# Batched attention-value product on one core: the loop of TensorE runs to the third unit from the end, and six of nine held stores go to the ring of SyncE

## The chip, the cores and the metric

One core of a Trainium2 chip. The metric is the device time of one execution in microseconds (us). A profiled execution has a span that is 1.8 us shorter than its time; moments below ("at 1046.2") count from the start of that span. "Landing" means a semaphore step that a DMA engine makes when its part of a transfer is done; a transfer over 16 engines makes 16, and the trace records each, without the engine's number.

In the views PE is TensorE, PEld its weight loads, DVE VectorE, ACT ScalarE, POOL GpSimd and SP SyncE (a q after the name: its queue of instructions), and L129 is line 129 of the kernel. The *ring* or *queue* of an engine holds the transfers that it has issued. GpSimd's *drain* (`pool.drain()`) is the last instruction of its program before the closing barrier.

## The reference

```python
batch, n_heads, seq, head_dim = 8, 12, 1024, 64      # float32
return np.einsum('bhqs,bhsd->bhqd', attn_weights, v)
```

The attention weights are 403 MB, v and the output 25 MB each.

## The kernel before

Two heads make a unit; there are NP = 48. GpSimd loads a unit with a cast to bf16 into one of two buffers. TensorE transposes it (64 matmuls of 128x128), VectorE and ScalarE copy the transposes out of PSUM, TensorE spreads v over the partitions by small matmuls and multiplies. A *plain* unit multiplies with v stationary, and its result is transposed back a unit later. A *direct* unit (the last three) multiplies group by group with the transposed weights stationary, so its result needs no transpose back and leaves in pieces.

```python
DIRECT = NP - 3          # units 45, 46, 47 are direct
LOOPED = DIRECT - 1      # units 2 to 43 in TensorE's loop, 0, 1 and 44 written out
HELD = 9                 # stores of units 38 to 46 wait behind the last loads
pieces_of = {NP - 4: [(0, GH), (GH, GH)], NP - 3: [(0, GH), (GH, GH)],
             NP - 2: [(0, 4), (4, 4), (8, 4), (12, 4)],
             NP - 1: [(0, 4), (4, 4), (8, 4), (12, 2), (14, 1), (15, 1)]}
last_stores = {4: (0, 8), 8: (8, 4), 12: (12, 2), 14: (14, 2)}
# ... (cut)
pe_pair(0, 1, 0, {0: (s_abf[0], 16)}, (s_vcast, 1), first=True)
pe_pair(1, 1, 1, {0: (s_abf[1], 16)}, None)
with nc.Fori(1, LOOPED // 2, 1, engines=(PE,)) as it:      # two units a turn
    # ...
for p in range(LOOPED, DIRECT): ...   pe_pair(...)         # unit 44
for p in range(DIRECT, NP):           pe_direct(p)         # units 45, 46, 47
# ... GpSimd:
for p in range(NP - 2):
    pool.wait_ge(s_t[True], (p + 1) * PER_DVE)   # unit p transposed: its buffer is free
    # ... v load after every odd unit
    load_attn(p + 2)
    if 0 < p <= HELD_FROM:
        store(p - 1)
for p in range(HELD_FROM, NP - 1):
    store(p)                                     # nine held stores, GpSimd's queue
pool.drain()
# ... SyncE: v's first load, four stores of unit 47, then waits for every store
```

Of the kernel before, what the change touches and what calls it, by code (L numbers as in the profile page):

```python
# [10 lines left out]
def kernel(  # L11
# [17 lines left out]
    nc = tc.nc  # L29
# [19 lines left out]

    DIRECT = NP - 3  # L50
    LOOPED = DIRECT - 1

    HELD = 9
    NO = HELD + 3
    pieces_of = {
        NP - 4: [(0, GH), (GH, GH)],
        NP - 3: [(0, GH), (GH, GH)],
        NP - 2: [(0, 4), (4, 4), (8, 4), (12, 4)],
        NP - 1: [(0, 4), (4, 4), (8, 4), (12, 2), (14, 1), (15, 1)],
    }  # L60

    groups_of = {p: [(0, 4), (4, 4), (8, 4), (12, 4)] for p in range(DIRECT, NP - 1)}
    groups_of[NP - 1] = [(0, 4), (4, 4), (8, 4), (12, 2), (14, 2)]
    last_stores = {4: (0, 8), 8: (8, 4), 12: (12, 2), 14: (14, 2)}
# [8 lines left out]
    def sem(name):  # L73
        return tc.alloc_semaphore(name)
# [8 lines left out]
    with tc.tile_critical(no_gpsimd_drain=True):  # L83
# [6 lines left out]
        vr = sb("vr", [P, VB, SB * D], bf16)  # L90
        vr_last = sb("vr_last", [P, VB, SB * D], bf16)
        vbf = [sb(f"vbf{i}", [P, SB, 2, D], bf16) for i in range(2)]
# [8 lines left out]
        s_abf = [sem(f"s_abf{i}") for i in range(2)]  # L101
        s_piece = {(p, n): sem(f"s_piece{p}_{n}") for p in pieces_of for n in range(len(pieces_of[p]))}
        s_v0, s_v, s_vlast = sem("s_v0"), sem("s_v"), sem("s_vlast")
        s_osb = [sem(f"s_osb{i}") for i in range(NO)]
# [6 lines left out]

        s_cp = [[sem(f"s_cp{i}_{g}") for g in range(G - 4)] for i in range(2)]
        s_vbf = [[sem(f"s_vbf{i}_{h}") for h in range(2)] for i in range(2)]
        s_ot = [[sem(f"s_ot{i}_{h}") for h in range(2)] for i in range(2)]

        s_c = {True: sem("s_c_dve"), False: sem("s_c_act")}
        s_out, s_od, s_oa = sem("s_out"), sem("s_od"), sem("s_oa")
        s_memset, s_const, s_vcast = sem("s_memset"), sem("s_const"), sem("s_vcast")

        def vr_of(p):  # L120
            return vr_last if p // 2 == NV - 1 else vr

# [15 lines left out]

        def spread_v(i, source):

            for h in range(2):
                rows = ds((2 * i + h) * VP, VP)
                for b in range(VB):
                    last = pe.matmul(  # L144
                        out=po[h],
                        lhsT=spread[rows, b],
                        rhs=source[rows, b],
                        start=(b == 0),
                        stop=(b == VB - 1),
                    )  # L150
                last.then_inc(s_sp[h])
# [29 lines left out]

        def pe_pair(i, n, before, waits, wait_v, first=False):

            for g in range(G):
                if g in waits:
                    pe.wait_ge(*waits[g])
                if g >= 4:
                    pe.wait_ge(s_cp[i][g - 4], n)
                transpose_g(abf[i], g)
            if not first:  # L190
                for h in range(2):
                    pe.wait_ge(s_ot[1 - i][h], before)
            if wait_v is not None:
                pe.wait_ge(*wait_v)
            spread_v(i, vr)
            if not first:
                transpose_back()
            for h in range(2):
                pe.wait_ge(s_vbf[i][h], n)
            multiply(i)  # L200

        def pe_direct(p):
# [5 lines left out]
            def mul(g):  # L208
# [8 lines left out]
                if g == 0:  # L217
                    for h in range(2):
                        pe.wait_ge(s_vbf[i][h], p // 2 + 1)
                copied = (p - DIRECT) * (PER_DVE if on_dve(g) else PER_ACT) + count_of(g)  # L220
# [16 lines left out]
            for g in range(G):  # L237
                if g in starts:

                    if g % 4 == 0:  # L240
                        while done < g:
                            mul(done)
                            done += 1
                    pe.wait_ge(s_piece[p, starts[g]], 16)
                if p > DIRECT or g >= 4:
# [4 lines left out]
                if g == 3:  # L250
                    if p == DIRECT:
                        for h in range(2):
                            pe.wait_ge(s_ot[1 - i][h], (p - 1) // 2 + 1)
                    elif p == NP - 2:
                        pe.wait_ge(s_vlast, 16)
                    spread_v(i, vr_of(p))
                    if p == DIRECT:
                        transpose_back()
# [6 lines left out]

        def piece_waits(p):
            return {g0: (s_piece[p, n], 16) for n, (g0, gn) in enumerate(pieces_of[p])}

        pe.wait_ge(s_const, 1 + VH)
        pe_pair(0, 1, 0, {0: (s_abf[0], 16)}, (s_vcast, 1), first=True)  # L270
        pe_pair(1, 1, 1, {0: (s_abf[1], 16)}, None)
        with nc.Fori(1, LOOPED // 2, 1, engines=(PE,)) as it:
            n = pe.snap(it + 1)
            loaded = pe.snap(it * 16)
            twice = pe.snap(loaded + 16)
            pe_pair(0, n, it, {0: (s_abf[0], twice)}, (s_v, loaded))
            pe_pair(1, n, n, {0: (s_abf[1], twice)}, None)
        for p in range(LOOPED, DIRECT):
            wait_v = (s_v, 16 * (p // 2)) if p % 2 == 0 else None
            pe_pair(p % 2, p // 2 + 1, (p - 1) // 2 + 1, piece_waits(p), wait_v)  # L280
        for p in range(DIRECT, NP):
# [3 lines left out]
        def copies_of_pair(p, dve):  # L285
# [7 lines left out]
            def spread_copy():  # L293
                eng.wait_ge(s_sp[h], p + 1)
                copy(  # L295
                    out=vbf[i][:, :, h], in_=po[h].rearrange("p (k d) -> p k d", k=SB)
                ).then_inc(s_vbf[i][h])

# [15 lines left out]
            for g in range(G):  # L314
# [3 lines left out]
                if on_dve(g) == dve:  # L318
# [5 lines left out]
                    if direct:  # L324
                        ins.then_inc(s_c[dve])
                    elif g < G - 4:
                        ins.then_inc(s_cp[i][g])
                if direct and g == 3:
# [13 lines left out]
        def back_copies(p):  # L342
            halves = osb[p % NO].rearrange("p (half j) d -> p half j d", half=2)
            free_osb(nc.scalar, p)
            for n in range(2):
                nc.scalar.wait_ge(s_back, 2 * p + n + 1)
                last = nc.scalar.copy(  # L347
# [5 lines left out]
        def ot_copy(p, h):  # L353
# [4 lines left out]
                out=ot[:, :, h], in_=po[h].rearrange("p (j q) -> p j q", j=GH)  # L358
            ).then_inc(s_ot[p % 2][h])

        nc.vector.memset(ident, 0.0).then_inc(s_memset)
        nc.vector.memset(spread, 0.0).then_inc(s_memset)
        nc.vector.wait_ge(s_v0, 16)
        nc.vector.tensor_copy(out=vr, in_=v32).then_inc(s_vcast)
        for p in range(NP):
# [13 lines left out]
        def load_attn(p):  # L379
            for n, (g0, gn) in enumerate(pieces_of.get(p, [(0, G)])):  # L380
                pool.dma_start(  # L381
                    out=abf[p % 2][:, ds(g0, gn)].rearrange("p g s -> p (g s)"),
                    in_=attn_p[p][:, ds(g0 * S, gn * S)],
                ).then_inc(s_piece[p, n] if p in pieces_of else s_abf[p % 2], 16)

        def load_v(iv):
            pool.dma_start(  # L387
                out=vr_of(2 * iv).rearrange("p b x -> p (b x)"), in_=v_g[iv]
            ).then_inc(s_v if iv < NV - 1 else s_vlast, 16)

        def store(p):
            if p < DIRECT:
                pool.wait_ge(s_out, p + 1)
            else:
                for s in (s_od, s_oa):
                    pool.wait_ge(s, (p - DIRECT + 1) * len(groups_of[DIRECT]))
            pool.dma_start(  # L397
                out=out_p[p].rearrange("p g d -> p (g d)"),
                in_=osb[p % NO].rearrange("p g d -> p (g d)"),
                single_packet=True,  # L400
            ).then_inc(s_osb[p % NO], 16)

# [25 lines left out]
        for p in range(NP - 2):  # L428
            pool.wait_ge(s_t[True], (p + 1) * PER_DVE)
            if p % 2 == 1 and (p + 1) // 2 < NV - 1:  # L430
                pool.wait_ge(s_sp[1], p + 1)  # L431
                load_v((p + 1) // 2)
            load_attn(p + 2)
            if p == LOOPED - 1:
                load_v(NV - 1)
            if 0 < p <= HELD_FROM:
                store(p - 1)
        for p in range(HELD_FROM, NP - 1):
            store(p)
# [3 lines left out]
        nc.sync.dma_start(out=v32.rearrange("p b x -> p (b x)"), in_=v_g[0]).then_inc(s_v0, 16)  # L443
        base = (NP - 1 - DIRECT) * len(groups_of[DIRECT])
        for k, (g0, gn) in enumerate(groups_of[NP - 1]):
            if g0 in last_stores:
                for s in (s_od, s_oa):
                    nc.sync.wait_ge(s, base + k + 1)
                gs = ds(*last_stores[g0])
                nc.sync.dma_start(  # L450
                    out=out_p[NP - 1][:, gs], in_=osb[(NP - 1) % NO][:, gs]
                ).then_inc(s_end, 16)
        for p in range(NP - 1 - NO, NP - 1):
            nc.sync.wait_ge(s_osb[p % NO], 16 * (p // NO + 1))
        nc.sync.wait_ge(s_end, 16 * len(last_stores))

# [29 lines left out]
```

## Time and profile before

| | before |
|---|---|
| time, median of the first three runs | 1059.7 us (1059.06 to 1059.75) |
| span of the profiled run | 1057.9 us |
| HBM read and written | 427.82 + 25.17 MB |
| TensorE busy | 75% |

The prediction below shows the lines that carry the reading. In the queue table a row is "queue kind: packets, MB, share of 16 engines". q0 is GpSimd's queue and q1 SyncE's. In the same table of the page of before:

```profile
q8 instruction: 9, 0.15, 0.1%
```

Those are nine packets of 16 KB. That they are TensorE's code is an inference: they come and go with the length of TensorE's program, as the experiments show.

### The profile page before, as it was taken

The page shows a single profiled execution, that of the slowest core. Times are in us where ns is not written, and L with a number is a line of the kernel's source. Part 1 is how long each engine was busy: PE and PEld are TensorE (multiplying, and loading weights), DVE is VectorE, ACT ScalarE, POOL GpSimd, SP SyncE. Part 2 cuts the span into 40 slices and gives each one's busy share as a digit, 9 for nine tenths or more (in the row PEclk, how much of TensorE's full clock was granted, in tenths as well). Part 3 has the DMA queues.
Part 4 walks back from the last instruction along what each step waited for, and adds up shares of the span by engine and source line. Part 5 has one row for each costly group of instructions (what it writes and reads, how often), then busy time and mean ns, then how long its engine had stood idle before and what let it go on. Part 6 is the DMA issues. An engine that isn't in the chain of part 4 may idle for free.

```text
span 1057.9 us, 12833 instructions
## 1 busy us (share of the span) xinstructions
PE 791.0 (75%) x5640; PEld 634.7 (60%) x5640; DVE 391.8 (37%) x589; ACT 397.3 (38%) x485; POOL 71.0 (7%) x137
## 2 busy tenths in 40 slices
PE   0896687866878678776787777876878768787995
PEld 0775476645755567555675556655666547656785
DVE  0443343333433334433353333433344334344452
ACT  0343343433433334433343333433344334344542
POOL 1010000100001000000000000000001000000020
PEclk9898888888889888898898888988789888898998
DMA  9999999999999999999999999999999999999997
GB/s 218 219 219 217 237 232 223 223 228 243 219 233 222 228 231 234 221 234 228 231 221 234 221 236 232 223 223 227 242 222 231 223 235 224 217 218 216 212 217 255
DMA packets 19171, 239.84 MB, mean 227 GB/s; under 512 B 2128, under 2 KB 2512, under 8 KB 11984
## 3 DMA queue, kind: packets, MB, share of 16 engines
q0 software_dynamic: 18432, 238.03, 100.1%
q1 hardware_dynamic: 720, 1.57, 0.4%
q8 instruction: 9, 0.15, 0.1%
q14 instruction: 10, 0.08, 0.0%
HBM read 427.82 MB, written 25.17 MB: 428 GB/s over the span
## 4 chain that ended last, share of the span: by engine, by line
DMA 66%; PE 29%; issue 1%; POOL 1%; ACT 1%; DVE 0%; POOLq 0%; SPq 0%
DMA abf<-in_attn_weights_dram 66%; PE bank L129 23%; PE bank L144 2%; PE bank L225 2%; POOL vr L387 1%; PE bank L172 1%; ACT at L320 0%; PE bank L156 0%; DVE vbf L295 0%; DVE at L320 0%; DVE osb L307 0%; ACT osb L347 0%; ACT vbf L295 0%; POOL abf L381 0%; POOLq L431 0%
## 5 line engine op out<-in xcount | busy, mean ns | idle before, releaser
L129 PE MATMUL bank<-ident,abf 128*128 128x128 f32 x3072 | 465.0, 322 | 249.7 <-DMA abf<-in_attn_weights_dram 249.7
L129 PEld LDWEIGHTS bank<-ident,abf 128*128 128x128 f32 x3072 | 453.0, 215 | 272.0 <-DMA abf<-in_attn_weights_dram 246.5
L320 DVE COPY at<-bank 128x1024 bf16<-128x1024 bf16 x480 | 320.5, 689 | 469.6 <-PE bank L129 466.1
L320 ACT COPY at<-bank 128x1024 bf16<-128x1024 bf16 x288 | 289.2, 1012 | 421.0 <-PE bank L129 421.0
L172 PE MATMUL bank<-at,vbf 128*64 128x512 bf16 x1440 | 216.5, 391 | 0.8 <-DVE vbf L295 0.8
L172 PEld LDWEIGHTS bank<-at,vbf 128*64 128x64 bf16 x1440 | 106.5, 108 | 96.2 <-DVE vbf L295 7.7
L357 ACT COPY ot<-bank 128x512 f32<-128x512 f32 x45 | 26.4, 587 | 183.7 <-PE bank L172 183.7
L357 DVE COPY ot<-bank 128x512 f32<-128x512 f32 x45 | 31.1, 692 | 144.5 <-PE bank L172 144.5
L381 POOL DMA_DIRECT2D abf<-in_attn_weights_dram x58 | 31.0, 539 | 423.8 <-PE bank L129 422.5
L156 PEld LDWEIGHTS bank<-ident,ot 128*128 128x128 f32 x360 | 38.5, 140 | 19.1 <-issue 19.1
L156 PE MATMUL bank<-ident,ot 128*128 128x128 f32 x360 | 49.2, 280 | 0.0
L347 ACT COPY osb<-bank 128x512 f32<-128x512 f32 x90 | 48.3, 589 | 0.3
L144 PE MATMUL bank<-vr,spread 32*128 32x512 bf16 x368 | 48.1, 377 | 0.0
L387 POOL DMA_DIRECT2D vr<-in_v_dram x22 | 11.6, 527 | 474.0 <-PE bank L144 474.0
L295 DVE CAST vbf<-bank 128x512 bf16<-128x512 f32 x48 | 33.2, 692 | 14.6 <-PE bank L144 14.6
L295 ACT CAST vbf<-bank 128x512 bf16<-128x512 f32 x48 | 28.1, 586 | 22.3 <-PE bank L144 22.2
L225 PE MATMUL bank<-vbf,at 128*128 128x128 bf16 x384 | 26.4, 219 | 4.4 <-DVE vbf L295 1.9
L397 POOL DMA_DIRECT2D out_dram<-osb x47 | 25.1, 543 | 59.5 <-ACT osb L347 48.3
L225 PEld LDWEIGHTS bank<-vbf,at 128*128 128x128 bf16 x384 | 22.9, 98 | 7.3 <-issue 2.9
L144 PEld LDWEIGHTS bank<-vr,spread 32*128 32x128 bf16 x368 | 15.4, 92 | 15.7
L307 DVE COPY osb<-bank 64x256 f32<-64x256 f32 (+1 forms) x13 | 5.1, 395 | 20.5 <-PE bank L225 20.5
L307 ACT COPY osb<-bank 64x256 f32<-64x256 f32 (+1 forms) x13 | 4.6, 351 | 20.6 <-PE bank L225 20.6
(13 smaller groups left out, 9.8 us busy)
## 6 DMA issues: line engine op xcount, KB each, us to landing
abf<-in_attn_weights_dram POOLq DMA_DIRECT2D x44, 4096.0 KB, 32.3
out_dram<-osb POOLq DMA_DIRECT2D x47, 512.0 KB, 32.3
vr<-in_v_dram POOLq DMA_DIRECT2D x22, 512.0 KB, 12.7
abf<-in_attn_weights_dram POOLq DMA_DIRECT2D x4, 2048.0 KB, 25.8
abf<-in_attn_weights_dram POOLq DMA_DIRECT2D x7, 1024.0 KB, 24.4
v<-in_v_dram SPq DMA_DIRECT2D x1, 1024.0 KB, 4.7
vr_last<-in_v_dram POOLq DMA_DIRECT2D x1, 512.0 KB, 30.3
abf<-in_attn_weights_dram POOLq DMA_DIRECT2D x1, 512.0 KB, 26.4
```

Of the source, the lines that this page charges most:

```text
L129: last = pe.matmul(out=pt[g % 4][:, k], lhsT=words[:, k], rhs=ident, is_transpose=True, start=(k == 0), stop=(k == KW - 1),)
L144: last = pe.matmul(out=po[h], lhsT=spread[rows, b], rhs=source[rows, b], start=(b == 0), stop=(b == VB - 1),)
L156: last = pe.matmul(out=px[n][:, ds(j * P, P)], lhsT=ot[:, 4 * n + j].rearrange("p h q -> p (h q)"), rhs=ident, is_transpose=True, start=(j ...
L172: last = pe.matmul(out=po[h][ds(half * D, D)], lhsT=vbf[i][:, 2 * kw + par, h], rhs=at[:, ds(half * GH, GH), kw, ds(h * HP, HP), par], sta ...
L225: last = pe.matmul(out=x[:, g - g0], lhsT=at[:, g, kw, :, par], rhs=vbf[i][:, 2 * kw + par].rearrange("p h d -> p (h d)"), start=(n == 0), ...
L295: copy(out=vbf[i][:, :, h], in_=po[h].rearrange("p (k d) -> p k d", k=SB)).then_inc(s_vbf[i][h])
L320: ins = copy(out=at[:, g].rearrange("c k j two -> c (k j two)"), in_=bank[g % 4].bitcast(bf16),)
L347: last = nc.scalar.copy(out=halves[:, :, ds(4 * n, 4)].rearrange("p half j d -> p j half d"), in_=px[n].rearrange("p (j half d) -> p j hal ...
L357: copy(out=ot[:, :, h], in_=po[h].rearrange("p (j q) -> p j q", j=GH)).then_inc(s_ot[p % 2][h])
L381: pool.dma_start(out=abf[p % 2][:, ds(g0, gn)].rearrange("p g s -> p (g s)"), in_=attn_p[p][:, ds(g0 * S, gn * S)],).then_inc(s_piece[p, n ...
L387: pool.dma_start(out=vr_of(2 * iv).rearrange("p b x -> p (b x)"), in_=v_g[iv]).then_inc(s_v if iv < NV - 1 else s_vlast, 16)
L397: pool.dma_start(out=out_p[p].rearrange("p g d -> p (g d)"), in_=osb[p % NO].rearrange("p g d -> p (g d)"), single_packet=True,).then_inc( ...
```

## The change

Intent: fewer units written out for TensorE, and a tail in which GpSimd's own stores are over early. The loop now covers units 0 to 45; 46 is plain and written out; only 47 is direct. Units 44 and 45 are loaded whole, 46 in two halves. V loads are announced to TensorE by SyncE. Of the nine held stores, GpSimd keeps three; SyncE issues six once the fourth piece of unit 47 (groups 12 and 13) has landed.

```diff
-    DIRECT = NP - 3
-    LOOPED = DIRECT - 1
+    DIRECT = NP - 1
+    LOOPED = NP - 2
     HELD = 9
+    BY_SYNC = NP - 1 - HELD + 3
+    GATE = 3
     pieces_of = {
-        NP - 4: [(0, GH), (GH, GH)],
-        NP - 3: [(0, GH), (GH, GH)],
-        NP - 2: [(0, 4), (4, 4), (8, 4), (12, 4)],
+        NP - 2: [(0, GH), (GH, GH)],
         NP - 1: [(0, 4), (4, 4), (8, 4), (12, 2), (14, 1), (15, 1)],
... (cut: one semaphore per purpose instead of one per parity; one v buffer instead of two)
-        pe_pair(0, 1, 0, {0: (s_abf[0], 16)}, (s_vcast, 1), first=True)
-        pe_pair(1, 1, 1, {0: (s_abf[1], 16)}, None)
-        with nc.Fori(1, LOOPED // 2, 1, engines=(PE,)) as it:
+        with nc.Fori(1, LOOPED // 2 + 1, 1, engines=(PE,)) as it:
... (cut)
+        for h in range(2):
+            nc.vector.memset(ot[:, :, h], 0.0).then_inc(s_ot[h])
... (cut)
-        for p in range(HELD_FROM, NP - 1):
+        for p in range(HELD_FROM, BY_SYNC):
             store(p)
         pool.drain()
... (cut)
+        for iv in range(1, NV):
+            nc.sync.wait_ge(s_v, 16 * iv)
+            nc.sync.sem_inc(s_vr)
+        nc.sync.wait_ge(*s_piece[NP - 1, GATE])
+        for p in range(BY_SYNC, NP - 1):
+            store(p, by_sync=True)
```

More of the change, by code (lines that the diff above doesn't have):

```diff
@@ L47 @@
     NV = NH // VH
-    DIRECT = NP - 3
-    LOOPED = DIRECT - 1
+    DIRECT = NP - 1
+    LOOPED = NP - 2
     HELD = 9
+    BY_SYNC = NP - 1 - HELD + 3
     NO = HELD + 3
+    GATE = 3
     pieces_of = {
-        NP - 4: [(0, GH), (GH, GH)],
-        NP - 3: [(0, GH), (GH, GH)],
-        NP - 2: [(0, 4), (4, 4), (8, 4), (12, 4)],
+        NP - 2: [(0, GH), (GH, GH)],
         NP - 1: [(0, 4), (4, 4), (8, 4), (12, 2), (14, 1), (15, 1)],
     }
-    groups_of = {p: [(0, 4), (4, 4), (8, 4), (12, 4)] for p in range(DIRECT, NP - 1)}
-    groups_of[NP - 1] = [(0, 4), (4, 4), (8, 4), (12, 2), (14, 2)]
+    groups_of = {NP - 1: [(0, 4), (4, 4), (8, 4), (12, 2), (14, 2)]}
     last_stores = {4: (0, 8), 8: (8, 4), 12: (12, 2), 14: (14, 2)}
@@ L90 @@
         vr = sb("vr", [P, VB, SB * D], bf16)
-        vr_last = sb("vr_last", [P, VB, SB * D], bf16)
         vbf = [sb(f"vbf{i}", [P, SB, 2, D], bf16) for i in range(2)]
@@ L101 @@
         s_abf = [sem(f"s_abf{i}") for i in range(2)]
-        s_piece = {(p, n): sem(f"s_piece{p}_{n}") for p in pieces_of for n in range(len(pieces_of[p]))}
-        s_v0, s_v, s_vlast = sem("s_v0"), sem("s_v"), sem("s_vlast")
+        s_piece = {
+            (p, n): (s_abf[p % 2], 16 * (p // 2 + 1)) if n == 0 else (sem(f"s_piece{p}_{n}"), 16)
+            for p in pieces_of
+            for n in range(len(pieces_of[p]))
+        }
+        s_v0, s_v = sem("s_v0"), sem("s_v")
         s_osb = [sem(f"s_osb{i}") for i in range(NO)]
@@ L110 @@
         s_back, s_x = sem("s_back"), sem("s_x")
-        s_cp = [[sem(f"s_cp{i}_{g}") for g in range(G - 4)] for i in range(2)]
-        s_vbf = [[sem(f"s_vbf{i}_{h}") for h in range(2)] for i in range(2)]
-        s_ot = [[sem(f"s_ot{i}_{h}") for h in range(2)] for i in range(2)]
+        s_cp = [sem(f"s_cp{g}") for g in range(G - 4)]
+        s_vbf = [sem(f"s_vbf{h}") for h in range(2)]
+        s_ot = [sem(f"s_ot{h}") for h in range(2)]
         s_c = {True: sem("s_c_dve"), False: sem("s_c_act")}
         s_out, s_od, s_oa = sem("s_out"), sem("s_od"), sem("s_oa")
-        s_memset, s_const, s_vcast = sem("s_memset"), sem("s_const"), sem("s_vcast")
-        def vr_of(p):
-            return vr_last if p // 2 == NV - 1 else vr
+        s_memset, s_const, s_vr = sem("s_memset"), sem("s_const"), sem("s_vr")
         pe = nc.tensor
@@ L137, in transpose_g, with spread_v @@
             last.then_inc(s_t[on_dve(g)])
-        def spread_v(i, source):
+        def spread_v(i):
             for h in range(2):
@@ L146, in spread_v @@
                         lhsT=spread[rows, b],
-                        rhs=source[rows, b],
+                        rhs=vr[rows, b],
                         start=(b == 0),
@@ L180, in multiply, with pe_pair @@
                 last.then_inc(s_m[h])
-        def pe_pair(i, n, before, waits, wait_v, first=False):
+        def pe_pair(i, n, waits, wait_v):
             for g in range(G):
@@ L187, in pe_pair @@
                 if g >= 4:
-                    pe.wait_ge(s_cp[i][g - 4], n)
+                    pe.wait_ge(s_cp[g - 4], n)
                 transpose_g(abf[i], g)
-            if not first:
-                for h in range(2):
-                    pe.wait_ge(s_ot[1 - i][h], before)
+            for h in range(2):
+                pe.wait_ge(s_ot[h], n)
             if wait_v is not None:
                 pe.wait_ge(*wait_v)
-            spread_v(i, vr)
-            if not first:
-                transpose_back()
+            spread_v(i)
+            transpose_back()
             for h in range(2):
-                pe.wait_ge(s_vbf[i][h], n)
+                pe.wait_ge(s_vbf[h], n)
             multiply(i)
@@ L218, in mul @@
                     for h in range(2):
-                        pe.wait_ge(s_vbf[i][h], p // 2 + 1)
+                        pe.wait_ge(s_vbf[h], p + 1)
                 copied = (p - DIRECT) * (PER_DVE if on_dve(g) else PER_ACT) + count_of(g)
@@ L243, in pe_direct @@
                             done += 1
-                    pe.wait_ge(s_piece[p, starts[g]], 16)
+                    pe.wait_ge(*s_piece[p, starts[g]])
                 if p > DIRECT or g >= 4:
@@ L252, in pe_direct @@
                         for h in range(2):
-                            pe.wait_ge(s_ot[1 - i][h], (p - 1) // 2 + 1)
-                    elif p == NP - 2:
-                        pe.wait_ge(s_vlast, 16)
-                    spread_v(i, vr_of(p))
+                            pe.wait_ge(s_ot[h], p + 1)
+                    spread_v(i)
                     if p == DIRECT:
@@ L264, in pe_direct @@
                 done += 1
-        def piece_waits(p):
-            return {g0: (s_piece[p, n], 16) for n, (g0, gn) in enumerate(pieces_of[p])}
         pe.wait_ge(s_const, 1 + VH)
-        pe_pair(0, 1, 0, {0: (s_abf[0], 16)}, (s_vcast, 1), first=True)
-        pe_pair(1, 1, 1, {0: (s_abf[1], 16)}, None)
-        with nc.Fori(1, LOOPED // 2, 1, engines=(PE,)) as it:
-            n = pe.snap(it + 1)
+        with nc.Fori(1, LOOPED // 2 + 1, 1, engines=(PE,)) as it:
             loaded = pe.snap(it * 16)
-            twice = pe.snap(loaded + 16)
-            pe_pair(0, n, it, {0: (s_abf[0], twice)}, (s_v, loaded))
-            pe_pair(1, n, n, {0: (s_abf[1], twice)}, None)
+            second = pe.snap(it * 2)
+            first = pe.snap(second - 1)
+            pe_pair(0, first, {0: (s_abf[0], loaded)}, (s_vr, it))
+            pe_pair(1, second, {0: (s_abf[1], loaded)}, None)
         for p in range(LOOPED, DIRECT):
-            wait_v = (s_v, 16 * (p // 2)) if p % 2 == 0 else None
-            pe_pair(p % 2, p // 2 + 1, (p - 1) // 2 + 1, piece_waits(p), wait_v)
+            waits = {g0: s_piece[p, n] for n, (g0, gn) in enumerate(pieces_of[p])}
+            pe_pair(p % 2, p + 1, waits, (s_vr, p // 2 + 1) if p % 2 == 0 else None)
         for p in range(DIRECT, NP):
@@ L296, in spread_copy @@
                     out=vbf[i][:, :, h], in_=po[h].rearrange("p (k d) -> p k d", k=SB)
-                ).then_inc(s_vbf[i][h])
+                ).then_inc(s_vbf[h])
             def out_copy(n):
@@ L326, in copies_of_pair @@
                     elif g < G - 4:
-                        ins.then_inc(s_cp[i][g])
+                        ins.then_inc(s_cp[g])
                 if direct and g == 3:
@@ L345, in back_copies @@
             for n in range(2):
-                nc.scalar.wait_ge(s_back, 2 * p + n + 1)
+                nc.scalar.wait_ge(s_back, 2 * (p + 1) + n + 1)
                 last = nc.scalar.copy(
@@ L358, in ot_copy @@
                 out=ot[:, :, h], in_=po[h].rearrange("p (j q) -> p j q", j=GH)
-            ).then_inc(s_ot[p % 2][h])
+            ).then_inc(s_ot[h])
         nc.vector.memset(ident, 0.0).then_inc(s_memset)
         nc.vector.memset(spread, 0.0).then_inc(s_memset)
+        for h in range(2):
+            nc.vector.memset(ot[:, :, h], 0.0).then_inc(s_ot[h])
         nc.vector.wait_ge(s_v0, 16)
-        nc.vector.tensor_copy(out=vr, in_=v32).then_inc(s_vcast)
+        nc.vector.tensor_copy(out=vr, in_=v32).then_inc(s_vr)
         for p in range(NP):
@@ L383, in load_attn, with store @@
                     in_=attn_p[p][:, ds(g0 * S, gn * S)],
-                ).then_inc(s_piece[p, n] if p in pieces_of else s_abf[p % 2], 16)
+                ).then_inc(s_abf[p % 2] if n == 0 else s_piece[p, n][0], 16)
         def load_v(iv):
             pool.dma_start(
-                out=vr_of(2 * iv).rearrange("p b x -> p (b x)"), in_=v_g[iv]
-            ).then_inc(s_v if iv < NV - 1 else s_vlast, 16)
-        def store(p):
-            if p < DIRECT:
-                pool.wait_ge(s_out, p + 1)
-            else:
-                for s in (s_od, s_oa):
-                    pool.wait_ge(s, (p - DIRECT + 1) * len(groups_of[DIRECT]))
-            pool.dma_start(
+                out=vr.rearrange("p b x -> p (b x)"), in_=v_g[iv]
+            ).then_inc(s_v, 16)
+        def store(p, by_sync=False):
+            eng = nc.sync if by_sync else pool
+            eng.wait_ge(s_out, p + 1)
+            eng.dma_start(
                 out=out_p[p].rearrange("p g d -> p (g d)"),
                 in_=osb[p % NO].rearrange("p g d -> p (g d)"),
-                single_packet=True,
-            ).then_inc(s_osb[p % NO], 16)
+                **({} if by_sync else {"single_packet": True}),
+            ).then_inc(s_end if by_sync else s_osb[p % NO], 16)
         load_attn(0)
@@ L429 @@
             pool.wait_ge(s_t[True], (p + 1) * PER_DVE)
-            if p % 2 == 1 and (p + 1) // 2 < NV - 1:
+            if p % 2 == 1:
                 pool.wait_ge(s_sp[1], p + 1)
@@ L433 @@
             load_attn(p + 2)
-            if p == LOOPED - 1:
-                load_v(NV - 1)
             if 0 < p <= HELD_FROM:
                 store(p - 1)
-        for p in range(HELD_FROM, NP - 1):
+        for p in range(HELD_FROM, BY_SYNC):
             store(p)
@@ L443 @@
         nc.sync.dma_start(out=v32.rearrange("p b x -> p (b x)"), in_=v_g[0]).then_inc(s_v0, 16)
-        base = (NP - 1 - DIRECT) * len(groups_of[DIRECT])
+        for iv in range(1, NV):
[4 more added lines that the diff above has]
+            store(p, by_sync=True)
         for k, (g0, gn) in enumerate(groups_of[NP - 1]):
@@ L447 @@
                 for s in (s_od, s_oa):
-                    nc.sync.wait_ge(s, base + k + 1)
+                    nc.sync.wait_ge(s, k + 1)
                 gs = ds(*last_stores[g0])
@@ L452 @@
                 ).then_inc(s_end, 16)
-        for p in range(NP - 1 - NO, NP - 1):
+        for p in range(BY_SYNC - NO, BY_SYNC):
             nc.sync.wait_ge(s_osb[p % NO], 16 * (p // NO + 1))
-        nc.sync.wait_ge(s_end, 16 * len(last_stores))
+        nc.sync.wait_ge(s_end, 16 * (NP - 1 - BY_SYNC + len(last_stores)))
 _INS = ['attn_weights', 'v']
```

## The prediction

> **What bounds the kernel now.** I read the page's table of 40 slices and its queue table first, since a kernel that reads 403 MB may be a transfer and little else; then the waits; then the timeline and stretches of the last 100 us, where the change acts.
>
> ```profile
> DMA  9999999999999999999999999999999999999997
> GB/s 218 219 219 217 237 232 223 223 228 243 219 233 222 228 231 234 221 234 228 231 221 234 221 236 232 223 223 227 242 222 231 223 235 224 217 218 216 212 217 255
> ...
> q0 software_dynamic: 18432, 238.03, 100.1%
> q1 hardware_dynamic: 720, 1.57, 0.4%
> ...
> HBM read 427.82 MB, written 25.17 MB: 428 GB/s over the span
> ```
>
> The DMA row is 9 in every slice but the last. The engines move 453 MB in 1057.9 us and never run dry; the lower GB/s row counts loads at their bf16 size, half of what is read. Busy PE (75%) is mostly waiting room.
>
> ```profile
> PE bank L129 <- DMA abf<-in_attn_weights_dram: 249.7, 44, 25.1
> ...
> SPq L454 <- DMA out_dram<-osb: 7.4, 5, 2.3
> SPq L83 <- POOLq L83: 1.9, 1, 1.9
> ```
>
> TensorE waits 44 times for a load. The chain of waits says it too (two thirds of the span is loads), but it follows the last compute copy at 1045.9 and says nothing of the final 12 us. The SP lines do: SP waits for stores, then 1.9 us for GpSimd.
>
> ```profile
> 957.73 10.10 PE L129 MATMUL bank<-ident,abf 128*128 128x128 f32 x64 [7.15 <-DMA abf<-in_attn_weights_dram]
> ...
> 974.50 8.02 PE L129 MATMUL bank<-ident,abf 128*128 128x128 f32 x64
> ...
> 989.24 0.99 PE L129 MATMUL bank<-ident,abf 128*128 128x128 f32 x6
> ```
>
> These are units 43, 44 and the first direct one, 45. After an idle gap of 7.15 us the 64 transposes take 10.1 us, without one 8.0. From 957.7 TensorE hardly stops, until it ends at 1045.9.
>
> ```profile
> 1038.00:1050.00 12.00, 7.65 (x94) 7.08 (x92) 4.33 (x9) 3.96 (x7) 0.00 (x0) 0.92 1.04 400
> 1050.00:1054.00 4.00, 0.00 (x0) 0.00 (x0) 0.00 (x0) 0.00 (x0) 0.00 (x0) 0.50 0.40 155
> 1054.00:1058.00 4.00, 0.00 (x0) 0.00 (x0) 0.00 (x0) 0.00 (x0) 0.00 (x0) 0.50 0.00 0
> ```
> ```profile
> L440 POOLq DRAIN  x1: 27720/27720/27720, 1028.8 to 1028.8; - x1
> ```
>
> In these stretches (columns: PE, PEld, DVE, ACT, POOL, clock, DMA share, GB/s) the DMA engines are full to 1050, partly busy to 1054, then idle for 4 us in which nothing computes. The trace's landing records say which transfer is last: the ninth held store (unit 46), issued at 1028.79, reports from the first engine at 1050.62 and from the last at 1054.12; the last of SP's four final stores landed at 1052.38. GpSimd's drain, started at 1028.77, lasts 27.72 us, to 1056.49: 2.37 us past the last landing of its own stores. SP is through its waits at 1054.4. So the end is: held stores drain (1054.1), GpSimd's drain (1056.5), closing barrier (1.4 us, to 1057.9).
>
> **What the Trainium skill says.** "DMA: Bandwidth & Descriptors", section "Where 436 GB/s comes from", puts the SBUF port ceiling at 435.2 GB/s. The trace agrees: 428 over the span, 98% of it. Its section "Issuing engines are not separate DMA queues" says transfers from SP and GpSimd share the same 16 engines and interleave. The trace agrees: SP's 64 KB stores landed a median 5.8 us after issue although GpSimd's stores had a backlog, and the sum stayed at 400 GB/s. "SWDGE vs HWDGE vs iDMA" in the same page says GpSimd's core builds descriptors in software while SP's are built by hardware; here a GpSimd issue takes 0.54 us and an SP issue 0.33. "TensorE: Matmul & The Clock Gate", section "What's actually happening", gives half clock after some 3.4 us of idleness; the 10.1 against 8.0 us above, and the 0.50 clock after TensorE stops, agree.
>
> **The change part by part.**
>
> *Rolling the start into the loop.* The first two units gain a transpose back of zeros, 8 matmuls, 1.1 us in the first. The second load lands at 45.3, and the first unit's PE work ends near 42, so it hides. The zeroing of ot is two VectorE operations in the time before v arrives at 5.7. Value: 0. Fewer instructions to fetch: the two instruction queues carry 0.23 MB, 0.1% of the engines. Value: below 0.3 us.
>
> *V through SP.* Each v load's arrival is passed on by SP. In the before kernel a v load trails the load issued ahead of it by 2.4 us (977.00, 979.46), while the unit that needs it still has 8 us of transposes. The added hop lies in that slack. The last v moves from before unit 46's load to before unit 47's: same bytes ahead of the last load. Value: 0.
>
> *Bytes and the last load.* Nine stores stay held, so the same bytes precede the last attention piece, which lands at 1040.9 now. The queue must not run dry. Unit 47's load is issued when 45's transposes are over: I work out 1010.9 below, against 1010.4 now, and the load ahead of it (unit 46) lands near 1018.8 (1021.2 less the 2.4 us of v that now comes later). Eight us of backlog: no gap. Value: 0.
>
> *TensorE's tail.* Units 44 and 45 are now loaded whole, so each start waits for its last byte. 44 starts at 977.04 instead of 974.50. Plain unit, warm: 8.0 transposes + 1.0 spread + 1.0 back + 4.75 multiply = 14.75, to 991.8. 45 waits for 998.85 (7 us, cold: 10.0 transposes): 16.75, to 1015.6. 46 is plain: 14.75, to 1030.35; its second half is wanted at 1019.6 and lands at 1018.8, its v near 1021.2, wanted at 1023.6. 47 is the only direct unit: unit 47 now takes 1027.83 to 1045.87, 18.04 us, and the transpose back with ScalarE's two copies, seen in the present first direct unit (1.8 us from spread to first multiply against 0.92), adds 0.9: to 1049.3. All its pieces have landed by the time they are wanted. So TensorE ends 3.4 us later: two idle gaps cost 9.5 us with 2 for the cold clock, and two direct units made plain give back about 9. Last store issued near 1049.6, against 1046.2.
>
> *Six stores on SP's ring.* SP issues after piece 12-13 lands (1038.3 now), six issues at 0.33 us, done by about 1041. GpSimd keeps three behind the loads. The backlog is the same 4.7 MB, on the same engines, at some 400 GB/s; the four final stores now queue behind six of their own ring. I estimate the last landing at 1053.3: the DMA floor of before (1050.6 to 1054.1 over the engines), with half to one us less because GpSimd's row alone made the late end, and because the last store issued at 1049.6 needs at least 2.3 us alone (SP's v load: 4.7 us for 1 MB, of which 2.4 are the bytes) and so fits.
>
> *The drain.* GpSimd's third store lands about 1047, its drain ends near 1049.5, before SP is done. The 1.9 us wait goes. From the last landing to the end there remain 0.55 (SP's waits, barrier) + 1.35 = 1.9 us.
>
> Sum of the span: 1053.3 + 1.9 = 1055.2, against 1054.1 + 3.8 = 1057.9: minus 2.7. Timed less profiled span was 1.8 us, so 1057.0. I add 0.3 for the tightness of TensorE's tail: 1057.3.
>
> **The rivals.**
>
> *TensorE becomes the end.* Its slack is some 1.5 us. If the cold unit costs 2 us more, or a copy stalls the direct unit, the last store goes out at 1052 and lands at 1054.5 to 1055. Against it: each term above is a measured duration. For it: three units in a row, nothing to absorb an error. It would make 1058.5 to 1059.5.
>
> *SP's stores drain worse.* They are not sent as single packets, and share the rings with the last two loads from 1039. If they run at 380 instead of 400 GB/s, 3.1 MB costs 0.4 us; if a slow engine is slow on both rings, no gain but the drain's. Then 1058.
>
> *They drain better.* The spread between first and last engine grew from 2.7 us (unit 47's first piece) to 3.5 in the held stores; if that belongs to GpSimd's descriptors, the end comes at 1052 and TensorE's store sets it: 1055.5.
>
> *The drain does not follow its own stores*, but the queues as a whole. Then 1.9 us stay: 1059.2.
>
> **Range and chances.** The DMA-fed 1038 us of the span are untouched, so all play is in the last 15 us: the rivals run from 1055.5 to 1059.5. Predicted 1057.3, eight in ten between 1055.0 and 1060.0. Two per cent is 21 us, more than the whole tail holds, so within 2% gets 0.985, faster 0.005, slower 0.01 for a starved queue.
>
> **What would show it.** Right: DMA still 9 in all slices; 64 cold transposes near 999; TensorE's last copy near 1049.5; GpSimd's drain over before SP's last wait, no SP wait for GpSimd; the last store landing near 1053. Wrong: a hole in the DMA row near 1011 to 1020 (load 47 late), a TensorE end past 1052, a share below 0.9 before 1050 (SP's stores late or slow), or a drain that still ends 2 us after SP.

## The result, and the profile after

The changed kernel took 1056.82 us (median of 4 runs, 1056.75 to 1056.89), the kernel before 1059.72 in the same rounds (4 runs, 1059.06 to 1059.91). The ratio is 0.9974, 95% interval 0.9956 to 0.9991. A ratio here is the mean time of one kernel's runs over that of the other's of the same rounds, so it is not quite the ratio of the medians. By the rule of 2% that is "the same", with a real gain of 2.9 us. The outputs are correct.

From the page of after, the DMA row of the 40 slices and the queue table:

```profile
DMA  9999999999999999999999999999999999999998
...
q0 software_dynamic: 16992, 234.89, 99.5%
q1 hardware_dynamic: 1584, 4.72, 1.2%
q8 instruction: 4, 0.07, 0.0%
...
HBM read 427.82 MB, written 25.17 MB: 429 GB/s over the span
```

The same bytes, no slice below 8, 3.1 MB moved from q0 to q1, and four code packets where there were nine. The waits of SyncE after:

```profile
SPq L389 <- DMA abf<-in_attn_weights_dram: 17.0, 1, 17.0
SPq L443 <- ACT osb L299: 7.4, 4, 3.9
SPq L450 <- DMA out_dram<-osb: 2.8, 1, 2.8
```

The first is the gate. The line of before in which SyncE waited 1.9 us for GpSimd is gone. The last stretches of after, columns as in the prediction (PE, PEld, DVE, ACT, POOL, clock, DMA share, GB/s):

```profile
1038.00:1050.00 12.00, 11.26 (x139) 10.60 (x138) 6.56 (x12) 5.30 (x8) 0.00 (x0) 1.00 1.03 408
1050.00:1054.00 4.00, 0.00 (x0) 0.00 (x0) 0.00 (x0) 0.00 (x0) 0.00 (x0) 0.75 0.28 97
```
```profile
1051.00:1052.00 1.00, 0.00 (x0) 0.00 (x0) 0.00 (x0) 0.00 (x0) 0.00 (x0) 0.98 0.29 99
1052.00:1053.00 1.00, 0.00 (x0) 0.00 (x0) 0.00 (x0) 0.00 (x0) 0.00 (x0) 0.50 0.08 27
```

Full to 1050, then a thinning tail. A share of 0.08 of 16 engines is little more than one engine at work. The DMA records end at 1052.94, the last landing is at 1053.28, and the span ends at 1055.0. GpSimd's drain, and TensorE's units 44 to 46 and its last multiply:

```profile
L430 POOLq DRAIN  x1: 32563/32563/32563, 1016.3 to 1016.3; - x1
```
```profile
976.97 9.37 PE L130 MATMUL bank<-ident,abf 128*128 128x128 f32 x64 [2.27 <-DMA abf<-in_attn_weights_dram]
...
998.75 10.28 PE L130 MATMUL bank<-ident,abf 128*128 128x128 f32 x64 [5.67 <-DMA abf<-in_attn_weights_dram]
...
1015.70 8.02 PE L130 MATMUL bank<-ident,abf 128*128 128x128 f32 x64
...
1047.89 1.57 PE L224 MATMUL bank<-vbf,at 128*128 128x128 bf16 x24
```

The drain runs from 1016.30 to 1048.87; GpSimd's last store had landed at 1046.90. TensorE ends 3.6 us later than before, at 1049.5, and the last store leaves SyncE at 1049.84 instead of 1046.23.

So the sum came out as predicted. Whether for the predicted reasons, the runs had to say.

### The profile page after: what moved, and what is told of

Same layout as the page of the kernel before. It is cut to its first block, busy times and chain, and to the rows that moved or that the text cites. A ratio compares the mean times of both kernels' runs of the same rounds, so it can differ in the third digit from the quotient of the medians. Undisturbed runs are those within 1.5% of the kernel's fastest.

```text
span 1055.0 us, 12504 instructions
## 1 busy us (share of the span) xinstructions
PE 791.8 (75%) x5472; PEld 631.6 (60%) x5472; DVE 390.7 (37%) x585; ACT 397.6 (38%) x483; POOL 65.8 (6%) x127
## 4 chain that ended last, share of the span: by engine, by line
DMA 69%; PE 27%; issue 1%; POOL 1%; ACT 0%; POOLq 0%; DVE 0%; SPq 0%
DMA abf<-in_attn_weights_dram 69%; PE bank L130 23%; PE bank L145 2%; POOL vr L382 1%; PE bank L173 1%; PE bank L224 1%; ACT at L312 0%; PE bank L157 0%; ACT osb L339 0%; ACT vbf L287 0%; POOL abf L376 0%; POOLq L423 0%; DVE osb L299 0%; POOLq L476 0%; SPq L84 0%
## 5 line engine op out<-in xcount | busy, mean ns | idle before, releaser
L173 PE MATMUL bank<-at,vbf 128*64 128x512 bf16 x1504 | 226.1, 391 | 0.0
L173 PEld LDWEIGHTS bank<-at,vbf 128*64 128x64 bf16 x1504 | 111.2, 108 | 99.3 <-DVE vbf L287 7.6
L157 PEld LDWEIGHTS bank<-ident,ot 128*128 128x128 f32 x384 | 41.0, 140 | 20.3 <-issue 20.3
L157 PE MATMUL bank<-ident,ot 128*128 128x128 f32 x384 | 52.4, 280 | 0.0
L389 POOL DMA_DIRECT2D out_dram<-osb x41 | 22.0, 538 | 48.4 <-ACT osb L339 48.3
L224 PE MATMUL bank<-vbf,at 128*128 128x128 bf16 x128 | 8.6, 219 | 1.0 <-ACT osb L339 0.8
L224 PEld LDWEIGHTS bank<-vbf,at 128*128 128x128 bf16 x128 | 7.5, 98 | 1.7 <-ACT osb L339 1.0
L299 DVE COPY osb<-bank 64x256 f32<-64x256 f32 (+1 forms) x5 | 1.8, 361 | 6.4 <-PE bank L224 6.4
L299 ACT COPY osb<-bank 64x256 f32<-64x256 f32 (+1 forms) x5 | 1.6, 325 | 5.3 <-PE bank L224 5.3
```

Source lines behind the costliest of these rows:

```text
L157: last = pe.matmul(out=px[n][:, ds(j * P, P)], lhsT=ot[:, 4 * n + j].rearrange("p h q -> p (h q)"), rhs=ident, is_transpose=True, start=(j ...
L173: last = pe.matmul(out=po[h][ds(half * D, D)], lhsT=vbf[i][:, 2 * kw + par, h], rhs=at[:, ds(half * GH, GH), kw, ds(h * HP, HP), par], sta ...
L224: last = pe.matmul(out=x[:, g - g0], lhsT=at[:, g, kw, :, par], rhs=vbf[i][:, 2 * kw + par].rearrange("p h d -> p (h d)"), start=(n == 0), ...
L389: eng.dma_start(out=out_p[p].rearrange("p g d -> p (g d)"), in_=osb[p % NO].rearrange("p g d -> p (g d)"), **({} if by_sync else {"single_ ...
```

## The experiments

Every run gave correct outputs and was timed in five rounds against the kernel before (medians of before 1059.58 to 1059.62, so results of different rounds are set side by side). Eight edits start from the changed kernel, two from the kernel before, and one from another variant. "Theory" and "rival" are named in each expectation.

### The two halves apart: `b_sp` and `a_pool`

`b_sp` is the kernel before with SyncE's six stores (the main lines of the edit):

```diff
-        for p in range(HELD_FROM, NP - 1):
+        for p in range(HELD_FROM, BY_SYNC):        # BY_SYNC = 41
             store(p)
 ...
+        nc.sync.wait_ge(s_piece[NP - 1, GATE], 16)
+        for p in range(BY_SYNC, NP - 1):
+            store(p, by_sync=True)
```

> The kernel before with six of the nine held stores on SP's ring, gated as in the changed kernel; TensorE's units as before. Theory (the gain is all from the ring, and in the changed kernel TensorE's later end, last store issued 1049.8, costs part of it): TensorE ends at 1045.9 as before, SP's six stores land by 1050.2, its final four behind them by 1051.5, end near 1053.3, time 1055.0. Rival (the rolled loop and the plain units give part of the gain): at or above 1056.8.

Measured: 1057.62 us, ratio 0.9981 (0.9967 to 0.9995). The rival was nearer. `a_pool` is the changed kernel with all nine on GpSimd's queue:

```diff
-    BY_SYNC = NP - 1 - HELD + 3
+    BY_SYNC = NP - 1
```

> The changed kernel with all nine held stores on GpSimd's queue: the loop part alone. Theory: the drain comes back, last landing near 1054.1, GpSimd free at 1056.5, time 1059.7 (1059.2 to 1060.5). Rival (the loop part itself gains): 1057 to 1058.5.

Measured: 1058.25 us (1058.17 to 1058.44), against 1059.58 for before (1059.19 to 1059.91); the ratio is 0.9988, its interval 0.9974 to 1.0002. The two sets of runs do not overlap, though the interval touches 1. Here too the rival was nearer: the loop half gains by itself. From the traces:

| | before | `b_sp` | `a_pool` | after |
|---|---|---|---|---|
| last landing | 1054.12 | 1053.99 | 1053.30 | 1053.28 |
| GpSimd answers the closing barrier | 1056.53 | 1054.27 | 1055.18 | 1053.56 |
| span ends | 1057.9 | 1055.9 | 1056.4 | 1055.0 |

Moving stores to SyncE hardly moves the last landing (0.13 and 0.02 us); it frees GpSimd. The loop half moves the last landing by 0.8 and 0.7 us. It also shortens the closing block: from GpSimd's answer to the end of the span 1.58 us in `b_sp` and 1.41 after, 1.36 in before and 1.20 in `a_pool`. In the traces 0.13 us of that is the clearing of semaphores, of which the changed kernel has fewer (504 ns and 373 ns). In `a_pool` SyncE still waits for GpSimd, as before; the waits of SyncE in that run:

```profile
SPq L84 <- POOLq L84: 1.4, 1, 1.4
```

### What the drain costs: `b_nodrain` and `a_nodrain`

Both take out one line:

```diff
-        pool.drain()
```

> The kernel before without GpSimd's drain, nothing else. Theory (1.9 us of the gain are GpSimd's drain of its own late stores): 1059.7 - 1.9 = 1057.8; the last landing stays at 1054.1. Rival (the closing barrier or GpSimd's queue waits for the same thing anyway, and the gain comes from where the stores go): 1059.7.

Measured: 1062.07 us, ratio 1.0023 (1.0010 to 1.0037): slower than before, where both theory and rival had expected no loss. The landings end at 1054.30, and GpSimd answers the first barrier at 1054.64, as the theory said. Then comes the closing block, which has a drain of its own (median 188 ns, longest 4.7 us, first at 1054.7):

```profile
L480 POOLq DRAIN  x3: 51/188/4711, 1054.7 to 1060.4; - x3
```

The same in the changed kernel, where GpSimd's last store had landed at 1046.98, 6.7 us before the closing drain:

> The changed kernel without GpSimd's drain. Theory (a drain is work of GpSimd's own that starts when it is issued: in the kernel before without it, the closing block's drain took 4.71 us, from 1054.72, although every store had landed at 1054.30): the closing drain starts near 1053.6 and takes some 4.6 us, time 1056.8 + 4.6 = 1061.4. Rival (a drain only waits for landings, and here GpSimd's stores have landed 6 us before): 1056.8.

Measured: 1060.48 us, 3.7 above the changed kernel's 1056.82, and ratio 1.0008 (0.9995 to 1.0022) to before. The closing drain:

```profile
L475 POOLq DRAIN  x3: 51/153/3894, 1053.7 to 1058.4; - x3
```

So the drain is not only a wait for landings. It takes 3.9 to 4.7 us when it starts after them, and ends 1.8 to 2.4 us after the last of GpSimd's landings when it was started long before (the other eleven kernels). The written drain buys overlap; here it had to start early, and GpSimd's last transfer had to land early too.

### Does TensorE's end matter: `a_early` and `e_one`

```diff
-    LOOPED = NP - 2
+    LOOPED = NP - 4
     pieces_of = {
-        NP - 2: [(0, GH), (GH, GH)],
+        NP - 4: [(0, GH), (GH, GH)],
+        NP - 3: [(0, GH), (GH, GH)],
+        NP - 2: [(0, 4), (4, 4), (8, 4), (12, 4)],
```

> The changed kernel with units 44, 45 and 46 out of the loop (plain still) and loaded in 2, 2 and 4 pieces, so that TensorE starts each as its first piece lands. Theory (in the changed kernel the last store of TensorE's chain, issued at 1049.84 when the held stores have all landed by 1050.2, sets the end): TensorE ends near 1046.5, the final store lands by 1051.5, time about 1055.0. Rival (the held stores set the end): 1056.8, unchanged.

Measured: 1057.11 us (1056.99 to 1057.16), so not faster; slower than the changed kernel by 0.3. The last store left SyncE at 1047.64 instead of 1049.84, but the last landing was at 1053.50. SyncE's final wait took the time that TensorE gave back: 5.2 us here, 2.8 in the changed kernel.

```profile
SPq L452 <- DMA out_dram<-osb: 5.2, 1, 5.2
```

The rival was right: TensorE's end has slack. My next guess was that four small stores in a row at the end of SyncE's ring cost more than their bytes. `e_one` starts from `a_early`:

```diff
-    last_stores = {4: (0, 8), 8: (8, 4), 12: (12, 2), 14: (14, 2)}
+    last_stores = {14: (0, 16)}
```

> The variant with the early TensorE tail (units 44 to 46 out of the loop, in pieces) with unit 47 stored by one 512 KB store instead of four. Theory (each small store at the end of SP's ring costs about 0.45 us beyond its bytes, landing after landing; the ring, not TensorE, sets the end): last landing near 1052.3 instead of 1053.5, time near 1055.9. Rival A (bytes alone set the end): 1057.1 as with four. Rival B (the store is now issued too late for the ring's backlog): 1057.5 or more.

Measured: 1056.84 us (1056.76 to 1057.19), and the last landing at 1053.50 to the hundredth as with four stores. My guess fell. In the three us from 1050 the DMA share was 0.78, 0.39 and 0.11: at the end some two of the 16 engines work on when the others have nothing left.

This also showed a trap in my own reading. I had taken the landings of SyncE's stores as complete by 1050.2. They share one semaphore, so a late engine's steps for one store mix with early engines' steps for the next. Only the last step of all is safe.

### Why one engine is late: `a_unroll` and `a_half`

Landing records of the first loads show how engines come to be late. For each load, the moment of its first landing, then how much later the 14th, 15th and 16th were:

```
                     first     14th   15th   16th     new code packet at
before, unit 0       24.66     0.27   0.29   0.33
before, unit 1       44.01     0.28   0.33   1.29     41.5
before, unit 2       63.38     0.28   0.33   1.29
before, v load       65.83     0.37   1.24   1.31     63.6
before, unit 3       85.96     0.40   2.04   2.23
before, unit 4      106.53     1.49   2.09   2.28     92.1
after,  unit 0       25.05     0.33   0.34   0.39
after,  unit 1       44.37     0.35   0.39   1.95     44.3
after,  unit 2       63.72     0.38   1.35   1.93     63.6
after,  v load       66.18     0.42   1.30   1.31
after,  unit 3       86.01     0.39   1.86   1.91
after,  unit 4      106.56     0.61   1.92   1.96
```

All 16 engines are within 0.4 us at unit 0, before the first code packet. After each of these packets one more engine is 0.9 to 1.6 us behind the others at the next landings. Not all of the lag has a packet beside it: between the v load and unit 3, without one, the two late engines go from 1.2 or 1.3 us behind to 1.9 or more, in both kernels. The lag lasts: in before the slowest of sixteen is 2.2 us behind at unit 45 and 2.7 at the end of unit 46.

But this is not yet the 0.8 us of the loop half. In the changed kernel, with four packets, the slowest engine is 2.1 and 2.7 us behind at the same places, and the last load is complete at 1040.67 against 1040.86. Most of the gain opens behind the loads. From there to the last landing it takes 13.26 us in before, 13.14 in `b_sp` and 13.44 in `b_nodrain`; it takes 12.61 after, and 12.48 to 12.66 in the seven other kernels of the table below. The bytes in this stretch are the same, and each of the kernels has one code packet in it. What costs 0.5 to 0.8 us there, in the three kernels with the TensorE program of before alone, stays open.

What many packets do can be tested by writing the loop out. `a_unroll` lets TensorE's loop make one turn (units 0 and 1) and writes out units 2 to 46:

```diff
-    LOOPED = NP - 2
+    LOOPED = 2
     pieces_of = {
+        **{p: [(0, G)] for p in range(2, NP - 2)},
```

> The changed kernel with the loop cut to its first turn and units 2 to 46 written out, nothing else: about 44 more fetches of 16 KB of TensorE code by the DMA engines. Theory (each fetch holds one engine for 0.9 us and pushes its share of the loads back by about 0.7 us, a different engine each time; this is what the loop part saved in the tail): 44 x 0.7 / 16 = 1.9 us later at the last landing, time near 1058.7. Rival (the fetches fall into slack, and the loop part's 1.3 us are something else): 1056.8.

Measured: 1062.04 us, 5.2 above the changed kernel, ratio 1.0023 to before (1.0009 to 1.0036). The theory's sign was right and its size too small: I had shared the delay evenly over the engines. The slowest engine of the load that first lands at 716.9 is 5.9 us behind, against 1.9 in the changed kernel. The landings of the load that first lands at 739.90 fall in two: eight within 1.7 us of the first, and eight 3.9 to 5.9 us behind. So the delay went to half of the engines; the theory's sum over eight is 3.9 us, still less than the 5.6 us by which the last landing moved. The queue table of the run:

```profile
q8 instruction: 43, 0.70, 0.2%
```

`a_half` sets `LOOPED = NP - 22` with the same kind of entry in `pieces_of`:

> The changed kernel with units 26 to 45 written out behind a shorter loop, half of what was written out in the run that came to 1062.0. Theory (fetches of TensorE code delay the slowest DMA engine): about 20 more fetches, half of the 5.2 us, time near 1059.4 (1058.4 to 1060.5). Rival (something else about the written-out units near the start, or about the loop being gone at all): 1056.8, or 1062 again.

Measured: 1058.37 us (1058.20 to 1058.68), 1.6 above the changed kernel; the theory had said 2.6, and 1058.4 at the least. Its queue table:

```profile
q8 instruction: 22, 0.36, 0.1%
```

All kernels whose bytes and gate were as in before or after, by code packets:

| code packets | last landing (us) | kernels |
|---|---|---|
| 4 | 1053.28, 1053.30, 1053.36, 1053.35 | after, `a_pool`, `a_nodrain`, `a_1pkt` |
| 6 | 1053.50, 1053.50 | `a_early`, `e_one` |
| 9 | 1054.12, 1053.99, 1054.30 | before, `b_sp`, `b_nodrain` |
| 22 | 1054.91 | `a_half` |
| 43 | 1058.89 | `a_unroll` |

The order holds without exception, whichever ring carries the stores. That packets delay engines is shown by the two written-out kernels: their last loads are complete at 1042.26 and 1046.23 instead of 1040.67, and behind them the stores take 12.65 and 12.66 us, as in the changed kernel. That the five packets between before and after cost the 0.8 us is not shown, and the landings speak against it: the last loads differ by 0.2 us, and `a_half` with 22 packets has the short stretch behind them. The kernels with nine packets are also those with three direct units, a start that is written out, and v loads that TensorE itself waits for; no run takes these apart. Only the loads in pieces are ruled out, since `a_early` and `e_one` have them and the short stretch (12.59 and 12.48). Which engine a packet went to the trace does not say.

### The gate and the rings: `a_nogate`, `a_allsp`, `a_1pkt`

```diff
-        nc.sync.wait_ge(*s_piece[NP - 1, GATE])
```

> The changed kernel without the wait that holds SP's six stores until piece 12-13 has landed: five of them go out at about 1021 and share the rings with unit 47's loads, whose last lands up to 6 us later, near 1047. Theory (the bytes are the same, and TensorE wants that piece only near 1047.5): unchanged, 1056.3 to 1057.3. Rival (the loads of the last unit are on the path, the gate earns its place): TensorE's last store 3 us or more late, 1059 or more.

Measured: 1058.34 us (1058.30 to 1058.38), 1.5 above the changed kernel and between the two expectations. TensorE was hardly later: its last store left at 1050.29 instead of 1049.84. What came back was GpSimd's drain. With SyncE's stores in the rings early, GpSimd's last loads and three stores fell behind, the last of them landing at 1053.39, and its drain (39.42 us from 1015.9) ended at 1055.4. The waits of SyncE:

```profile
SPq L84 <- POOLq L84: 1.1, 1, 1.1
```

So the gate earns its place, though for a reason that neither theory nor rival named: it lets GpSimd's queue run out early.

`a_allsp` puts all nine on SyncE's ring:

```diff
-    BY_SYNC = NP - 1 - HELD + 3
+    BY_SYNC = NP - 1 - HELD
```

> The changed kernel with all nine held stores on SP's ring, none behind the loads on GpSimd's. Theory (the end is the bytes of the slowest DMA engine, on whichever ring): that engine has loads until the gate opens, so no hole for it and an end of 1056.8, at most 0.5 more. Rival (three stores on GpSimd's queue are needed to bridge from the last load to SP's first store): a hole of 1 us or more near 1039, time 1057.8 or more.

Measured: 1057.68 us (1057.60 to 1057.76), 0.9 above the changed kernel, nearly what the rival said. The stretch in which GpSimd's queue had run out and SyncE's first store was not yet under way:

```profile
1038.00:1039.00 1.00, 1.00 (x15) 0.99 (x13) 0.90 (x2) 0.42 (x1) 0.00 (x0) 1.00 0.39 72
```

A share of 0.39 for one us is a hole of 0.6 us; with three stores kept on GpSimd's queue the share in that stretch was 1.03 (in `a_1pkt`). The three are a bridge. `a_1pkt` sends SyncE's stores as single packets:

```diff
-                **({} if by_sync else {"single_packet": True}),
+                single_packet=True,
```

> The changed kernel with SP's six stores sent as single packets, as GpSimd's are. Theory (bytes of the slowest engine): unchanged, 1056.8 within 0.4. Rival (the order in which an engine takes turns between the rings decides when GpSimd's three stores land): they land earlier or later by 2 us or more, but as its drain ends 5 us before the end, the time stays 1056.8 all the same; only a worse drain of SP's own would show, 1057.5 or more.

Measured: 1056.77 us (1056.69 to 1056.95), unchanged, and GpSimd's last store landed at 1046.99 against 1046.90. That part of the change does nothing for the time.

No variant beats the changed kernel clearly: `a_1pkt` and `e_one` are within 0.1 us of it.

## Why the prediction was right, and where it was not

The time (1057.3 predicted, 1056.82 measured) and the span (1055.2 and 1055.0) were right; the 0.3 us added for TensorE's tail were not needed. The bulk of the gain, GpSimd's drain, was right in mechanism too. The rest of the sum was right by luck, as the last two points say. Step by step:

- **DMA is the bound, no hole at unit 47's load.** Right. The last load landed at 1040.67 after and 1040.86 before; I had said no difference. One reading does not hold: I set the 428 GB/s beside the port ceiling of SBUF and called it agreement. The 428 counts bytes at the HBM; what the page's packets moved, with loads at their bf16 size, is 239.84 MB or 227 GB/s. No run here shows that ceiling.
- **TensorE's tail.** Right almost to the hundredth where it counted: unit 46's transposes began at 1015.70 (1015.6 predicted), and TensorE's last matmul ended at 1049.46 (1049.3). One term was off: unit 44's transposes took 9.4 us, not 8.0, and the wait for unit 45 absorbed it. The granted clock was 0.50 from 976.88 to 980.29, after a gap of 2.27 us. I had counted the unit as warm; the clock section that the prediction cites speaks of some 3.4 us of idleness, and here 2.27 us were enough. That TensorE's end sets nothing was right too, as `a_early` and `e_one` show.
- **The drain.** Right: the 1.9 us wait went (the drain was predicted to end at 1049.5, and ended at 1048.87); `b_sp` shows it alone, 2.0 us of time. The rival that the drain follows the queues as a whole fell. So did the two on the rate of SP's stores: 408 GB/s against 400 in the stretch from 1038 to 1050, and a last landing that the ring alone moves by 0.13 us.
- **Rolling the start into the loop, "below 0.3 us".** This is the term that was mis-sized, with the zeros that I gave to the plain units' bytes and to v's way through SP: together the loop half is worth 1.3 us alone (`a_pool`) and 0.8 beside the ring (`b_sp` against after). Some 0.2 us each are the shorter closing block and the earlier end of the loads; the larger part opens behind the loads, and its cause is open. To read "0.1% of the engines", an average over 16, was also wrong in kind, since the end belongs to the slowest engine: `a_unroll` loses 5.2 us with 0.2%.
- **Six stores on SP's ring, last landing 1053.3 "because GpSimd's row alone made the late end".** The number was right (1053.28) and the reason wrong: with the ring alone the last landing stays at 1053.99. The two errors, nothing for the loop and some 0.8 us for the ring, cancelled in the sum. That was luck.

The gains do not add: 2.0 alone for the ring, 1.3 for the loop, 2.9 together in the first comparison, since the loop half alone also shortens the drain's part (from the last landing to GpSimd's answer 2.41 us in before, 1.88 in `a_pool`), which the ring removes anyway.

## What to carry to other kernels

Where DMA is the bound, ask which engine ends last, not how busy the sixteen are: in a queue that hardly empties, what delays single engines adds up to the end, and written-out code did that here (5.2 us for 39 packets). Give GpSimd a drain of its own early, and let its last transfer land some microseconds before the end; give the last stores to another queue. And check a sum by its parts: here two wrong terms made a right total, and only the 2x2 of the change's halves showed it. Then check the story of each half against the traces of both kernels: the late engine of before is as late in after.

## What the Trainium skill lacked or had wrong

- "Runtime: NRT & Kernel Launch", section "Instruction fetch mechanics", says crossing a 16 KiB boundary costs one tail-bump, "mostly hidden", and that kernels prefer full unrolling where possible. In this DMA-bound kernel a 16 KB code packet holds one DMA engine for 0.94 us (mean of nine in before) and leaves it 0.9 to 1.6 us behind the others; 39 more packets cost 5.2 us of 1057.
- "DMA: Bandwidth & Descriptors", section "Latency and other measured facts", has engines 7 and 15 usually slower, with the software descriptor rings as its best guess. Here all 16 engines were within 0.4 us for the first load, which was software-issued, and the late engines appeared with the code packets at 41.5 and 63.6 us, though their lag then grew from 1.3 to about 2 us without one. Which engines they were, the trace does not say.
- No page gives the cost of GpSimd's drain after its transfers: 3.9 to 4.7 us when it starts after the last landing, 1.8 to 2.4 us past the last landing when it starts early.
- "DMA: Bandwidth & Descriptors", section "Issuing engines are not separate DMA queues", says that several issuers save only issue time. For the rate that held (408 and 400 GB/s in the same stretch), but the choice of issuer was worth 2.0 us at the end (`b_sp`), by freeing GpSimd's drain.
